# Input projection with 512 moving columns, low parts shared with GpSimd, rotary scores in pairs, output units between head pairs

## The chip, the core and the metric

The kernel runs on one core of a Trainium2 chip. The metric is the device time of one execution in microseconds. Engines are named as in the profile: PE is TensorE's matmul, PEld its weight load, DVE is VectorE, ACT is ScalarE, POOL is GpSimd, SP is SyncE, whose queue issues the weight transfers.

## What is computed

One decoder layer over 256 positions of width 2048, all in float32:

```
x = LN(x)
h = x @ w_in                                   # 2048 -> 2368 columns
c_q, c_kv, k_rope, u_conv, u_pool = split(h)   # 512, 256, 64, 1024, 512
mla:  q = rms(c_q) @ w_uq, kv = rms(c_kv) @ w_ukv, rotary on 64 of 192,
      8 heads, causal softmax, values of 128
conv: a * sigmoid(g) -> causal depthwise conv, 31 taps -> LN -> swish
pool: trailing mean over 2/4/8/16 minus token -> linear per group -> scale
y = concat(mla, conv, pool) @ w_out ;  x = LN(alpha * x + y)
up = causal_conv3(x @ w_up) ; a, g = split(up) ; x = LN(alpha * x + (a * silu(g)) @ w_down)
```

## The kernel before

**Products in three parts.** A large product is made of float32r matmuls: each weight tile and each activation is cut into a high part (its float32r rounding) and a low part (the rest), and hi*hi, hi*lo and lo*hi are added in one PSUM bank. Attention, transposes and statistics use plain float32 matmuls; each of these stands in the trace as two records.

**Weight units.** All weights come as units of 128 x 2048 in a fixed list (`units`): 19 of `w_in` (8 conv, 2 kv, 1 rotary key, 4 q, 4 pool; the first two are used as plain float32), 2 of `w_ukv`, 3 of `w_uq`, 16 of `w_out`, 88 of `w_up`, 44 of `w_down`. A unit is loaded in two halves of 1024 columns. For each half, ScalarE writes the high part (`make_hi`, L198) and VectorE the low part by a subtraction (`make_lo`, L214). `take` hands out the next unit and stages two units further. High and low tiles have six buffers each, three units' worth.

**Input projection.** The channels of x lie in `X`, a tile per k-tile with 256 high and 256 low columns side by side (`X.wide`). `proj` takes for each k-tile and column block three matmuls of 256 moving columns, so that the bank holds the finished sum in its first 256 columns. `proj_wide`, used by the up-projection, takes one matmul over all 512 columns with the high weights, and one of 256 columns with the low weights; the two halves of the bank are added afterwards (`ffn_conv`). In the first unit of a pair it takes the high weights first, in the second the low ones.

**Work in the background.** The 31 taps of each of the four conv groups (L573, L576) go into a queue `bgq`; `bg(n)` takes n of them, and `NBG` sets n after each unit for the conv, kv/q, pool, `w_ukv`/`w_uq` and output units. What is left is done just before `conv_rows`, which transposes the conv groups' results (L818). The angles of the rotary embedding run on GpSimd from a queue of their own (`pq`, `pbg`).

**Attention.** `att_scores(h)` computes the scores of one head and its softmax. The rotary key lies twice, once in rows 0 to 63 (`KA`) and once in rows 64 to 127 (`KB`) with zeros elsewhere, because a tile of rotary queries holds two heads. Two heads ahead of the transposes, the scores are issued; units of the output projection (`wo_unit`) stand between heads in two places. Output units have matmuls of 512 columns; eight banks of PSUM hold everything.

**First residual LayerNorm.** The last three output units are kept; for tokens 0 to 127 they are finished first, then `moments(0)`, and the transposes of the normalised rows (`ln_to_channels`, L277) are woven with the last output matmuls of tokens 128 to 255 (`weave0`). The up-projection's first matmuls (`up_high`, L915) fill the time until the second block's transposes. The reciprocal root of the variance is a power on GpSimd (L263).

**Order.** The program is written in the order in which it is to run; a planner with a cost table orders what is not pinned (`pin`) by readiness and place in the program.

Of the kernel before, what the change touches and what calls it, by code (L numbers as in the profile page):

```python
# [9 lines left out]
F32 = mybir.dt.float32  # L10
# [5 lines left out]
P = 128  # L16
# [22 lines left out]
NBG = (4, 4, 4, 4, 4)  # L39
# [43 lines left out]
def build(tc, ctx, a, out):  # L83
# [77 lines left out]
    wo_order = [(0, 3), (1, 3), (0, 0), (0, 1), (1, 0), (1, 1), (0, 2), (1, 2),  # L161
# [5 lines left out]
    LOOK = 2  # L167
    staged = deque()
# [13 lines left out]
    def stage_load(home=None, raws=None):  # L182
# [8 lines left out]
        for h in range(2):  # L191
# [151 lines left out]
    def m(name="m", dt=F32, w=S):  # L343
        return mp.tile([P, 288], dt, tag="m", name=nm(name), bufs=28)[:, 0:w]
# [169 lines left out]
    def proj(nun, kper, ncb, ah, al, banks, nbg=0, total=None):  # L514
        total = total or nun * kper
        for u in range(nun):
            w = take()
            for k in range(kper):
                kt = u * kper + k
                s0, s1 = kt == 0, kt == total - 1  # L520
                for cb in range(ncb):
                    c = (k * ncb + cb) * P
                    o = banks[cb][:, 0:S]
                    mm(o, w(0, c, P), ah[kt], s0, False)
                    mm(o, w(0, c, P), al[kt], False, False)
                    mm(o, w(1, c, P), ah[kt], False, s1)
            bg(nbg)
            pbg(6)

    def proj_wide(x, xh, banks, nbg=0, u0=0):  # L530
# [10 lines left out]
        for u in range(u0, 2):  # L541
# [10 lines left out]
            bg(nbg)  # L552

    def split_ps(ps, scale, hi, lo):
        act.activation(hi, ps, AF.Identity, scale=scale)
        dve.scalar_tensor_tensor(lo, ps, scale, hi.bitcast(F32), op0=mul, op1=sub)


    accs = []
    for j in range(4):  # L560
        ba, bg_ = first if j == 0 else (bank(), bank())
        if j:
            proj(2, 8, 2, xh, xl, [ba, bg_], nbg=NBG[0])
# [3 lines left out]
        act.activation(sig, bg_[:, 0:S], AF.Sigmoid)  # L567
        dve.tensor_tensor(hp[:, NCONV - 1:NCONV - 1 + S], ba[:, 0:S], sig, op=mul)
# [26 lines left out]
    proj(2, 8, 2, xh, xl, kvb, nbg=NBG[1])  # L595
    kvg, sqs = [], []
    for i in range(2):
        v = m("kvg")
        act.activation(v, kvb[i][:, 0:S], AF.Identity, scale=PC("kv_g", i))
        q = m("sq")  # L600
        act.activation(q, kvb[i][:, 0:S], AF.Square)
        kvg.append(v)
        sqs.append(q)
# [13 lines left out]
    rs_kv = token_rms(sqs, 256)  # L617
    diag = m("diag", w=S)
    for t in range(NTB):
        dve.tensor_scalar(diag[:, t * P:(t + 1) * P], ident, rs_kv[:, t:t + 1], None, op0=mul)  # L620
# [10 lines left out]
    KA = mp.tile([P, S], F32, tag="KA", name="KA")  # L631
    KB = mp.tile([P, S], F32, tag="KB", name="KB")
    pool.memset(KA[64:128], 0.0)
    pool.memset(KB[0:64], 0.0)


    qh, ql, qsq = [], [], []
    for c in range(2):
        qb = [bank(), bank()]
        proj(2, 8, 2, xh, xl, qb, nbg=NBG[1])  # L640
        if c == 0:
# [8 lines left out]
            dve.tensor_tensor(KA[0:64], t0_[0:64], t1_[0:64], op=add)  # L650
            dve.tensor_tensor(KB[64:128], t0_[64:128], t1_[64:128], op=add)
# [10 lines left out]
        for i in range(2):  # L662
            hh, ll = m("cqh", F32R), m("cql", F32R)
            split_ps(qb[i][:, 0:S], PC("q_g", c * 2 + i), hh, ll)
            q = m("sq")
            act.activation(q, qb[i][:, 0:S], AF.Square)
# [10 lines left out]
    def pool_group(gi, b):  # L677
# [4 lines left out]
        act.copy(up[:, PAD:PAD + S], b[:, 0:S])  # L682
# [51 lines left out]
    def q_unit(c):  # L734
        w = take()
        qs = []
        for i in range(4):
# [9 lines left out]
            qs.append(qn)  # L747
        bg(NBG[3])
# [3 lines left out]
    QN += q_unit(1)  # L752
    for i in range(4):
        rope(QR[i], COS, SIN)
# [13 lines left out]
    def att_scores(h):  # L768
        b = bank()
        krr = KA if h % 2 == 0 else KB  # L770
        qr = QR[h // 2]
        mm(b[:, 0:P], QN[h][:, 0:P], KN[h][:, 0:P], True, False)
        mm(b[:, 0:P], qr[:, 0:P], krr[:, 0:P], False, True)
        mm(b[:, P:P + S], QN[h][:, P:S], KN[h], True, False)
        mm(b[:, P:P + S], qr[:, P:S], krr, False, True)
        p = mp.tile([P, 512], F32, tag="p", name=nm("p"), bufs=3)
# [36 lines left out]
    def conv_rows():  # L813

        for t in range(NTB):
# [6 lines left out]
            yn = mp.tile([P, 512], F32, tag="p", name=nm("yn"), bufs=3)  # L822
# [42 lines left out]
    att_scores(0)  # L865
    att_scores(1)
    QN += q_unit(2)
    for i in range(2, H + 4):
        if i < H:
            att_scores(i)  # L870
        if i - 2 < H:
            att_transpose(i - 2)
        if i >= 4:
            att_out(i - 4)
        if i in (4, 7):
            wo_unit(0 if i == 4 else 1)
            bg(NBG[4])
    for i in range(2, 16 - NLAST):
# [51 lines left out]
    for i in range(NLAST):  # L930
# [5 lines left out]
    weave0 = [(1, (2,)), (1, (3,)), (2, (0,)), (2, (1, 2, 3))]  # L936
    ln_to_channels(0, mv, "ln1_g", "ln1_b", X1.pair, lambda w: m("v", w=w),
                   hooks=[(7, f) for f in his0 + his1], weave=lambda kq: last_out(1, weave0[kq][0], ks=weave0[kq][1]))
# [253 lines left out]
```

## Time and profile before

| | |
|---|---|
| median of 3 runs | 1016.16 us (1015.11 to 1016.96) |
| the profiled execution | 1014.3 us, its span 1012.5 us |
| TensorE matmul busy | 1003.0 us, 99% |
| weight loads busy | 884.4 us, 87% |
| VectorE busy | 703.3 us, 69% |
| ScalarE busy | 509.5 us, 50% |
| GpSimd busy | 52.5 us, 5% |
| mean granted TensorE clock | 0.998 |

Times in the trace count from the first instruction. A busy share is an average: which engine sets the end is seen from the chain of work that ended last. Records of matmuls overlap, so the time that a matmul costs is the distance from its start to the next one's start.

### The profile page before, as it was taken

The page shows a single profiled execution, that of the slowest core. Times are in us where ns is not written, and L with a number is a line of the kernel's source. Part 1 is how long each engine was busy: PE and PEld are TensorE (multiplying, and loading weights), DVE is VectorE, ACT ScalarE, POOL GpSimd, SP SyncE. Part 2 cuts the span into 40 slices and gives each one's busy share as a digit, 9 for nine tenths or more (in the row PEclk, how much of TensorE's full clock was granted, in tenths as well). Part 3 has the DMA queues.
Part 4 walks back from the last instruction along what each step waited for, and adds up shares of the span by engine and source line. Part 5 has one row for each costly group of instructions (what it writes and reads, how often), then busy time and mean ns, then how long its engine had stood idle before and what let it go on. Part 6 is the DMA issues. An engine that isn't in the chain of part 4 may idle for free.

```text
span 1012.5 us, 14976 instructions
## 1 busy us (share of the span) xinstructions
PE 1003.0 (99%) x5752; PEld 884.4 (87%) x5752; DVE 703.3 (69%) x1070; ACT 509.5 (50%) x751; POOL 52.5 (5%) x95
## 2 busy tenths in 40 slices
PE   9999999999999999999999999999999999999997
PEld 9999999888898888888888888888888888888885
DVE  6998589987699866666566666666665554554576
ACT  5545466454565654554555455545545444444440
POOL 0830230000000000000000000000000000000000
PEclk9999999999999999999999999999999999999999
DMA  8656444666178656565656555665655766566532
GB/s 322 220 189 197 167 143 148 172 225 206 65 244 253 208 189 197 179 193 189 197 181 195 189 189 188 188 196 181 198 188 191 268 193 204 188 189 201 191 127 84
DMA packets 55656, 193.16 MB, mean 191 GB/s; under 512 B 6432, under 2 KB 6688, under 8 KB 55328
## 3 DMA queue, kind: packets, MB, share of 16 engines
q1 hardware_dynamic: 55152, 191.86, 58.6%
q8 instruction: 45, 0.74, 0.3%
q10 hardware_dynamic: 432, 0.35, 0.1%
q14 instruction: 27, 0.22, 0.1%
HBM read 190.08 MB, written 2.10 MB: 190 GB/s over the span
## 4 chain that ended last, share of the span: by engine, by line
PE 97%; DVE 1%; ACT 1%; DMA 0%; POOL 0%; issue 0%; POOLq 0%; SPq 0%; ACTq 0%
PE ps L256 93%; PE ps L471 1%; PE ps L915 1%; DMA x<-in_x 0%; ACT v L287 0%; PE ps L461 0%; PE ps L586 0%; DVE st L449 0%; PE ps L277 0%; POOL mv L263 0%; PE ps L1069 0%; PE ps L625 0%; PE ps L759 0%; PE ps L1070 0%; DVE st L857 0%; DVE x L856 0%
## 5 line engine op out<-in xcount | busy, mean ns | idle before, releaser
L214 DVE TENSOR_TENSOR lo<-raw,hi 128x1024 fp32r<-128x1024 f32 x340 | 408.6, 1212 | 266.0 <-ACT hi L198 247.3
L198 ACT CAST hi<-raw 128x1024 fp32r<-128x1024 f32 (+1 forms) x342 | 355.4, 1043 | 399.5 <-PE ps L256 366.5
L256 PE MATMUL ps<-x,hi 128*128 128x512 f32 (+1 forms) x1888 | 412.9, 361 | 0.0
L256 PEld LDWEIGHTS ps<-x,hi 128*128 128x128 f32 x1888 | 335.4, 189 | 51.3
L256 PE MATMUL ps<-x,lo 128*128 128x256 f32 x1664 | 248.2, 283 | 0.0
L256 PEld LDWEIGHTS ps<-x,lo 128*128 128x128 f32 x1664 | 223.7, 192 | 3.3
L256 PE MATMUL ps<-hi,al 128*128 128x512 f32 x352 | 136.9, 389 | 0.0
L256 PE MATMUL ps<-hi,ah 128*128 128x512 f32 x352 | 136.9, 389 | 0.0
L256 PE MATMUL ps<-lo,ah 128*128 128x512 f32 x352 | 136.9, 389 | 0.0
L256 PE MATMUL ps<-hi,mx 128*128 128x512 f32 x256 | 81.2, 393 | 0.0
L256 PEld LDWEIGHTS ps<-hi,al 128*128 128x128 f32 x352 | 66.1, 188 | 13.8
L256 PEld LDWEIGHTS ps<-lo,ah 128*128 128x128 f32 x352 | 66.1, 188 | 13.7
L256 PEld LDWEIGHTS ps<-hi,ah 128*128 128x128 f32 x352 | 66.1, 188 | 13.6
L576 DVE SCALAR_TENSOR_TENSOR acc<-hp,pc,acc 128x256 f32<-128x256 f32 x120 | 59.1, 492 | 2.7
L256 PEld LDWEIGHTS ps<-hi,mx 128*128 128x128 f32 x256 | 48.1, 188 | 9.7
L263 POOL TENSOR_TENSOR mv<-mv,cc 128x1 f32<-128x1 f32 x8 | 6.0, 753 | 874.8 <-DVE mv L262 813.5
L256 PE MATMUL ps<-lo,mx 128*128 128x512 f32 x128 | 49.8, 389 | 0.0
L976 ACT COPY u<-ps 128x256 f32<-128x256 f32 x88 | 28.5, 377 | 22.0 <-PE ps L256 21.8
L977 DVE TENSOR_TENSOR u<-ps,u 128x256 f32<-128x256 f32 x88 | 32.9, 415 | 0.0
L256 PEld LDWEIGHTS ps<-lo,mx 128*128 128x128 f32 x128 | 24.1, 188 | 4.7
L978 ACT ACTIVATE ta<-u,pc 128x256 f32<-128x256 f32 x44 | 24.2, 602 | 1.1 <-DVE u L977 1.1
L978 ACT ACTIVATE tg<-u,pc 128x256 f32<-128x256 f32 x44 | 24.1, 600 | 0.1
(181 smaller groups left out, 662.0 us busy)
## 6 DMA issues: line engine op xcount, KB each, us to landing
raw<-in_w_up SPq DMA_DIRECT2D x174, 512.0 KB, 4.3
raw<-in_w_down SPq DMA_DIRECT2D x88, 512.0 KB, 4.2
raw<-in_w_in SPq DMA_DIRECT2D x34, 512.0 KB, 4.3
raw<-in_w_out SPq DMA_DIRECT2D x32, 512.0 KB, 4.5
raw<-in_w_uq SPq DMA_DIRECT2D x6, 512.0 KB, 4.0
x<-in_x SPq DMA_DIRECT2D x8, 256.0 KB, 5.4
plain<-in_w_in SPq DMA_DIRECT2D x4, 512.0 KB, 7.2
raw<-in_w_ukv SPq DMA_DIRECT2D x4, 512.0 KB, 4.1
```

What stands on the lines that cost most here:

```text
L198: i_ = act.copy(hi, raw[:, o:o + wd])
L214: i_ = dve.tensor_tensor(lo, raw[:, o:o + wd], w.parts[0][len(w.parts[1])].bitcast(F32), op=sub)
L256: pe.matmul(o, l, r, start=start, stop=stop)
L263: pool.tensor_tensor(mv[:, 2:3], mv[:, 1:2], nhalf[:, 0:1], op=ALU.pow)
L471: pin(pe.matmul(first[cb][:, t * P:(t + 1) * P], plain[kt // 8](((kt % 8) * 2 + cb) * P, P), vx[c][:, j, t * P:(t + 1) * P], start=kt == 0 ...
L576: dve.scalar_tensor_tensor(acc, hp[:, k:k + S], PC("conv_w", j * NCONV + k), acc, op0=mul, op1=add)
L915: pin(pe.matmul(token_block(ub[u // 2 * 2 + cb], t), us[u](0, up_col(kt, cb), P), token_block(X1.wide(kt), t), start=t == 0 and kt % 16 == ...
L976: act.copy(u, ps[:, S:2 * S])
L977: dve.tensor_tensor(u, ps[:, 0:S], u, op=add)
L978: act.activation(t_, u, AF.Identity, scale=PC("ffn_w", 2 * 2 * NF + blk), bias=PC("ffn_b", blk))
```

## The change

The conv (three of four groups), kv, q and pool projections use `proj_wide` and `halves`, which copies the second half of the bank and adds it to the first; `proj` goes. The low part of the second half of units 9 to 29 is computed by GpSimd. The kv statistics are taken in the middle of the first q projection. The four squares of q are added by GpSimd before one product with ones. The rotary key lies in one tile `KR`, its two copies in rows 0 to 63 and 64 to 127, and the rotary scores of two heads are products of 64 rows each. The rope of the queries runs between the heads of the next query unit. Scores and softmax go by pairs of heads, an output unit stands before each pair's transposes from the second pair on, and the order of two output units is swapped. In the first residual LayerNorm the output matmuls go behind the first two transposes, and one low part moves behind the fourth pair of channels. Scratch tiles `m` are 27 instead of 28, softmax tiles `p` 4 instead of 3.

```
-NBG = (4, 4, 4, 4, 4)
+NBG = (4, 5, 6, 4, 4)
-    wo_order = [(0, 3), (1, 3), (0, 0), (0, 1), (1, 0), (1, 1), (0, 2), (1, 2),
+    wo_order = [(0, 3), (1, 3), (0, 0), (1, 0), (0, 1), (1, 1), (0, 2), (1, 2),
+    POOL_LO = range(9, 30)
-            def make_lo(raw=raw, h=h, late=True):
+            def make_lo(raw=raw, h=h, late=True, eng=pool if h and nxt[0] - 1 in POOL_LO else dve):
-                    i_ = dve.tensor_tensor(lo, raw[:, o:o + wd], w.parts[0][len(w.parts[1])].bitcast(F32), op=sub)
+                    i_ = eng.tensor_tensor(lo, raw[:, o:o + wd], w.parts[0][len(w.parts[1])].bitcast(F32), op=sub)
-        return mp.tile([P, 288], dt, tag="m", name=nm(name), bufs=28)[:, 0:w]
+        return mp.tile([P, 288], dt, tag="m", name=nm(name), bufs=27)[:, 0:w]
-    def proj(nun, kper, ncb, ah, al, banks, nbg=0, total=None):
...
-    def proj_wide(x, xh, banks, nbg=0, u0=0):
+    def proj_wide(x, xh, banks, nbg=0, u0=0, npq=0, between=None):
...
             bg(nbg)
+            pbg(npq)
+            if u == 0 and between is not None:
+                between()
+    xw = [X.wide(k) for k in range(KT)]
+    def halves(b, dst=None):
+        t_ = m("half")
+        act.copy(t_, b[:, S:2 * S])
+        dst = t_ if dst is None else dst
+        dve.tensor_tensor(dst, b[:, 0:S], t_, op=add)
+        return dst
-            proj(2, 8, 2, xh, xl, [ba, bg_], nbg=NBG[0])
+            proj_wide(xw, xh, [ba, bg_], nbg=NBG[0], npq=6)
...
+        gate, val = (halves(bg_), halves(ba)) if j else (bg_[:, 0:S], ba[:, 0:S])
+        act.activation(sig, gate, AF.Sigmoid)
+        dve.tensor_tensor(hp[:, NCONV - 1:NCONV - 1 + S], val, sig, op=mul)
-    rs_kv = token_rms(sqs, 256)
...
+    def kv_diag():
+        rs_kv = token_rms(sqs, 256)
+        for t in range(NTB):
+            dve.tensor_scalar(diag[:, t * P:(t + 1) * P], ident, rs_kv[:, t:t + 1], None, op0=mul)
...
-        proj(2, 8, 2, xh, xl, qb, nbg=NBG[1])
+        proj_wide(xw, xh, qb, nbg=NBG[1], npq=6, between=kv_diag if c == 0 else None)
-            dve.tensor_tensor(KA[0:64], t0_[0:64], t1_[0:64], op=add)
-            dve.tensor_tensor(KB[64:128], t0_[64:128], t1_[64:128], op=add)
+            dve.tensor_tensor(KR, t0_, t1_, op=add)
...
-        proj(2, 8, 2, xh, xl, pb, nbg=NBG[2])
+        proj_wide(xw, xh, pb, nbg=NBG[2], npq=6)
         if c == 0:
-            rs_q = token_rms(qsq, 512)
+            for q in qsq[1:]:
+                pool.tensor_tensor(qsq[0], qsq[0], q, op=add)
+            rs_q = token_rms(qsq[0:1], 512)
...
-    QN += q_unit(1)
-    for i in range(4):
-        rope(QR[i], COS, SIN)
+    QN += q_unit(1, lambda i: rope(QR[i], COS, SIN))
...
+    def att_scores(h0):
+        hs = (h0, h0 + 1)
+        for h in hs:
+            SB[h] = bank()
+            mm(SB[h][:, 0:P], QN[h][:, 0:P], KN[h][:, 0:P], True, False)
+            mm(SB[h][:, P:P + S], QN[h][:, P:S], KN[h], False, False)
+        qr = QR[h0 // 2]
+        for o, q, nk in ((slice(0, P), slice(0, P), P), (slice(P, P + S), slice(P, S), S)):
+            for i, h in enumerate(hs):
+                r = slice(i * 64, (i + 1) * 64)
+                pin(pe.matmul(SB[h][:, o], qr[r, q], KR[r, 0:nk], start=False, stop=o.start == P))
...
+    def softmaxes(h0):
+        att_scores(h0)
+        att_softmax(h0)
+        att_softmax(h0 + 1)
+    softmaxes(0)
     QN += q_unit(2)
...
+    for h in range(0, H, 2):
+        if h + 2 < H:
+            softmaxes(h + 2)
+        if h:
+            wo_unit(h // 2 - 1)
             bg(NBG[4])
+        att_transpose(h)
+        att_transpose(h + 1)
+        if h:
+            att_out(h - 2)
+            att_out(h - 1)
+    att_out(H - 2)
+    att_out(H - 1)
-    for i in range(2, 16 - NLAST):
+    for i in range(3, 16 - NLAST):
...
-    weave0 = [(1, (2,)), (1, (3,)), (2, (0,)), (2, (1, 2, 3))]
+    def weave0(kq):
+        if kq == 0:
+            last_out(1, 1, ks=(2, 3))
+        elif kq == 1:
+            last_out(1, 2)
...
-    los0[0]()
...
-                   hooks=[(3, los0[1]), (7, los1[0]), (7, los1[1]), (7, los2[0]), (7, los2[1])], weave=weave1)
+                   hooks=[(3, los0[0]), (3, los0[1]), (7, los1[0]), (7, los1[1]), (7, los2[0]), (7, los2[1])], weave=weave1)
```

## Rows read from the trace of the kernel before

**Rows 1.** The page's first part: busy time, share of span, instructions.
```profile
PE 1003.0 (99%) x5752; PEld 884.4 (87%) x5752; DVE 703.3 (69%) x1070; ACT 509.5 (50%) x751; POOL 52.5 (5%) x95
```

**Rows 2.** The chain that ended last: start us, us, engine, line, count.
```profile
91.84 23.03 PE ps L256 x192
114.87 1.68 PE ps L586 x16
...
195.12 0.87 PE ps L818 x8
```

**Rows 3.** Timeline of TensorE in the up-projection, us 300 to 312: start, us, instructions merged.
```profile
302.77 7.44 PE L256 MATMUL ps<-x,hi 128*128 128x512 f32 x32
310.05 2.19 PE L256 MATMUL ps<-x,lo 128*128 128x256 f32 x17
```

**Rows 4.** Timeline of TensorE at the first heads' scores.
```profile
154.34 0.39 PE L256 MATMUL ps<-KA,qn 128*128 128x128 f32 x2
154.56 0.60 PE L256 MATMUL ps<-kn,qn 128*128 128x256 f32 x2
154.99 0.59 PE L256 MATMUL ps<-KA,qn 128*128 128x256 f32 x2
155.43 0.38 PE L256 MATMUL ps<-kn,qn 128*128 128x128 f32 x2
...
156.55 0.47 PE L256 MATMUL ps<-cqh,hi 128*128 128x256 f32 x1
156.85 0.28 PE L256 MATMUL ps<-cql,hi 128*128 128x256 f32 x1
```

**Rows 5.** Timelines of TensorE and of VectorE at the first pair.
```profile
27.27 0.48 PE L256 MATMUL ps<-x,hi 128*128 128x256 f32 x2
...
31.72 3.69 DVE L214 TENSOR_TENSOR lo<-raw,hi 128x1024 fp32r<-128x1024 f32 x3
```

**Rows 6.** Busy time from 60 to 195: all, of tile lo, of tile acc.
```profile
60.00:195.00 135.00, 135.00 (x993) 128.29 (x992) 117.04 (x257) 74.24 (x143) 16.18 (x30) 1.00 0.51 161
...
60.00:195.00 135.00, 77.53 (x262) 49.75 (x262) 44.94 (x38) 1.00 0.51 161
...
60.00:195.00 135.00, 0.04 (x1) 0.18 (x2) 48.73 (x101) 1.00 0.51 161
```

**Rows 7.** Timeline of VectorE: low parts and conv taps.
```profile
75.11 3.08 DVE L576 SCALAR_TENSOR_TENSOR acc<-hp,pc,acc 128x256 f32<-128x256 f32 x6
78.11 2.35 DVE L214 TENSOR_TENSOR lo<-raw,hi 128x1024 fp32r<-128x1024 f32 x2
...
129.22 2.88 DVE L576 SCALAR_TENSOR_TENSOR acc<-hp,pc,acc 128x256 f32<-128x256 f32 x4
```

**Rows 8.** Timeline of GpSimd at the pool groups' sums.
```profile
118.86 0.62 POOL L687 TENSOR_TENSOR ws<-up 128x258 f32<-128x258 f32 x1
...
128.36 1.43 POOL L687 TENSOR_TENSOR ws<-up 128x262 f32<-128x262 f32 x1 [7.34 <-ACT up L682]
129.87 1.44 POOL L687 TENSOR_TENSOR ws<-ws 128x260 f32<-128x260 f32 x2
```

**Rows 9.** Timelines of GpSimd, VectorE and TensorE at the first residual LayerNorm.
```profile
261.52 0.55 POOL L263 TENSOR_TENSOR mv<-mv,cc 128x1 f32<-128x1 f32 x1 [61.77 <-DVE mv L262]
272.48 1.39 POOL L263 TENSOR_TENSOR mv<-mv,cc 128x1 f32<-128x1 f32 x1 [10.41 <-DVE mv L262]
...
272.24 1.22 DVE L214 TENSOR_TENSOR lo<-raw,hi 128x1024 fp32r<-128x1024 f32 x1
...
269.35 3.99 PE L915 MATMUL ps<-x,hi 128*128 128x256 f32 x32
274.50 0.66 PE L277 MATMUL ps<-cc,x 128*128 128x128 f32 x4 [1.17 <-DVE x L272]
```

**Rows 10.** Timeline of VectorE at the last conv taps.
```profile
190.95 3.09 DVE L576 SCALAR_TENSOR_TENSOR acc<-hp,pc,acc 128x256 f32<-128x256 f32 x6
```

**Rows 11.** The page's fifth part: a group of instructions, busy us, mean ns.
```profile
L977 DVE TENSOR_TENSOR u<-ps,u 128x256 f32<-128x256 f32 x88 | 32.9, 415 | 0.0
```

More of the change, by code (lines that the diff above doesn't have):

```diff
@@ L511, in build @@
     res_in = residual_ops(dve, a["ln_in_g"], a["ln_in_b"])
-    def proj(nun, kper, ncb, ah, al, banks, nbg=0, total=None):
[L515 to L528, printed above, removed]
-    def proj_wide(x, xh, banks, nbg=0, u0=0):
+    def proj_wide(x, xh, banks, nbg=0, u0=0, npq=0, between=None):
         def high(w, kt, last):
@@ L594, in build @@
     kvb = [bank(), bank()]
-    proj(2, 8, 2, xh, xl, kvb, nbg=NBG[1])
+    proj_wide(xw, xh, kvb, nbg=NBG[1], npq=6)
     kvg, sqs = [], []
     for i in range(2):
+        kv = halves(kvb[i])
         v = m("kvg")
-        act.activation(v, kvb[i][:, 0:S], AF.Identity, scale=PC("kv_g", i))
+        act.activation(v, kv, AF.Identity, scale=PC("kv_g", i))
         q = m("sq")
-        act.activation(q, kvb[i][:, 0:S], AF.Square)
+        act.activation(q, kv, AF.Square)
         kvg.append(v)
@@ L615, in build @@
     cs_ = cos_sin()
-    rs_kv = token_rms(sqs, 256)
     diag = m("diag", w=S)
-    for t in range(NTB):
-        dve.tensor_scalar(diag[:, t * P:(t + 1) * P], ident, rs_kv[:, t:t + 1], None, op0=mul)
+    def kv_diag():
+        rs_kv = token_rms(sqs, 256)
+        for t in range(NTB):
+            dve.tensor_scalar(diag[:, t * P:(t + 1) * P], ident, rs_kv[:, t:t + 1], None, op0=mul)
     def rope(src, cos, sin):
@@ L629, in rope @@
         dve.tensor_tensor(src, src, t1, op=add)
[L631 to L634, printed above, removed]
+    KR = mp.tile([P, S], F32, tag="KA", name="KR")
     qh, ql, qsq = [], [], []
@@ L663, in build @@
             hh, ll = m("cqh", F32R), m("cql", F32R)
-            split_ps(qb[i][:, 0:S], PC("q_g", c * 2 + i), hh, ll)
+            qs_ = halves(qb[i])
+            split_ps(qs_, PC("q_g", c * 2 + i), hh, ll)
             q = m("sq")
-            act.activation(q, qb[i][:, 0:S], AF.Square)
+            act.activation(q, qs_, AF.Square)
             qh.append(hh)
@@ L681, in pool_group @@
         pool.memset(up[:, 0:PAD], 0.0)
-        act.copy(up[:, PAD:PAD + S], b[:, 0:S])
+        halves(b, up[:, PAD:PAD + S])
         cur, wdt = up, 1
@@ L733, in build, with q_unit @@
     bg(NBG[3])
-    def q_unit(c):
+    def q_unit(c, between=None):
         w = take()
@@ L747, in q_unit @@
             qs.append(qn)
+            if between is not None:
+                between(i)
         bg(NBG[3])
@@ L766, in build, with att_softmax @@
     SC, PT = {}, {}
[L768 to L776, printed above, removed]
+    SB = {}
+    def att_scores(h0):
[9 more added lines that the diff above has]
+                pin(pe.matmul(SB[h][:, o], qr[r, q], KR[r, 0:nk], start=False, stop=o.start == P))
+    def att_softmax(h):
+        b = SB.pop(h)
+        p = mp.tile([P, 512], F32, tag="p", name=nm("p"), bufs=4)
         sm = small(name="smx")
@@ L821, in conv_rows @@
             mv = ln_stats_finish(st, 1, t)
-            yn = mp.tile([P, 512], F32, tag="p", name=nm("yn"), bufs=3)
+            yn = mp.tile([P, 512], F32, tag="p", name=nm("yn"), bufs=4)
             dve.tensor_scalar(yn, b, mv[:, 0:1], mv[:, 2:3], op0=sub, op1=mul)
@@ L863, in wo_unit @@
             wo_mm(n, kg, w, t, kg == 3, False)
-    att_scores(0)
-    att_scores(1)
-    QN += q_unit(2)
[L868 to L876, printed above, removed]
-            bg(NBG[4])
-    for i in range(2, 16 - NLAST):
+    def softmaxes(h0):
[3 more added lines that the diff above has]
+    softmaxes(0)
+    QN += q_unit(2)
+    for h in range(0, H, 2):
[3 more added lines that the diff above has]
+            wo_unit(h // 2 - 1)
+            bg(NBG[4])
+        att_transpose(h)
[6 more added lines that the diff above has]
+    for i in range(3, 16 - NLAST):
         n, kg = wo_order[i]
@@ L935, in build @@
     last_out(1, 1, ks=range(2))
-    weave0 = [(1, (2,)), (1, (3,)), (2, (0,)), (2, (1, 2, 3))]
+    def weave0(kq):
[3 more added lines that the diff above has]
+            last_out(1, 2)
     ln_to_channels(0, mv, "ln1_g", "ln1_b", X1.pair, lambda w: m("v", w=w),
-                   hooks=[(7, f) for f in his0 + his1], weave=lambda kq: last_out(1, weave0[kq][0], ks=weave0[kq][1]))
+                   hooks=[(7, f) for f in his0 + his1], weave=weave0)
     for f in his2:
```

2 lines of the change are left out of this document (removed).

## The prediction

> **What bounds the kernel now.** I read the page first, then the chain that ended last, then timelines of single engines. TensorE is busy 99% of the span [rows 1], and the chain is a nearly unbroken row of its matmuls: 192 in 23.03 us, then sixteen small ones in 1.68 us, and so on [rows 2]. The reader is to see that only two things shorten this time: less TensorE work, or removal of one of its few waits. Inside the body I find one wait above 0.5 us: the transposes of the second token block at the first residual LayerNorm, 1.17 us idle [rows 9]. VectorE and GpSimd matter only if they come too late.
>
> **Input projection.** Before, each k-tile and column block takes three matmuls of 256 moving columns; 192 take 23.03 us, 0.120 each [rows 2]. After, one of 512 and one of 256. The up-projection already has both shapes: 32 of 512 columns start 7.28 us apart in all, 0.2275 each [rows 3]. So 0.3475 takes the place of 0.360, 0.0125 less. There are 8 projections (three conv, one kv, two q, two pool) of 16 k-tiles and 2 blocks, 256 such triples: **-3.2 us**. These are columns of the same number; what goes is one issue of three. I see no unknown in it.
>
> The new order has a cost. In a pair's second unit the low parts come first now. The first pair's matmuls begin at 27.27, so its second unit's begin 5.56 us later, at 32.83; but three low parts run on VectorE from 31.72 to 35.41 [rows 5], and the first two belong to that unit. They end, a third of the stretch each, at about 33.0 and 34.2, while TensorE wants them at 32.8 and, eight matmuls on, at 33.8. **+0.5 us** (0 to 0.6); later units are further ahead.
>
> **Halves added.** Sixteen additions on VectorE, each like the up-projection's 415 ns [rows 11], and as many copies on ScalarE (four replace others). They sit behind a bank that TensorE does not need at once, since the next pair takes other banks. Nothing on the path; VectorE gets 10 x 0.34 (one after another they overlap a little) = 3.4 us more between 60 and 195 us.
>
> **Sums of squares of q.** Sixteen records at 1.68 us [rows 2] become four: **-1.26 us**. GpSimd adds the four tiles while the first pool projection runs (11 us of matmuls); its three additions, 0.62 each at 258 columns [rows 8], end long before. The kv statistics move into the middle of the first q projection, with 5.5 us of matmuls before the result is used; the chain behind them is some 2 us plus one low part on GpSimd. Nothing on the path.
>
> **Rotary scores.** Now two heads share a zero-padded 128-row product each. From 154.34 to 154.56 the 128-column part takes 0.22, from 154.99 to 155.43 the 256-column part 0.44 [rows 4]: 0.66 per head, 5.25 us for eight. After, two heads' products use rows 0-63 and 64-127. No row shows 64-row products. Bounds: two halves wholly at once, -2.6; one after the other, 0, plus eight changes of shape. For a change of shape the nearest row is the first low-precision matmul behind the scores, 0.30 instead of 0.12 [rows 4], 0.18; eight would be +1.4. Each f32 product is two records, issued in order: with first-head-first order only the second record of one head can meet the first of the other, so I take a third, -1.75, less eight half-priced changes, 0.7: **-1.0** (-2.6 to +1.4).
>
> The Trainium skill ("TensorE: Matmul & The Clock Gate", Part 3) says that matmuls in distinct row groups run concurrently, starting some 4 ns apart; by it this term would be the full -2.6. Its page "TensorEngine Tiling (Array Packing)", Key Properties, says that a change of tiling mode drains the engine, which speaks the other way; no row here shows either.
>
> **Rope between query heads.** The same eight records, but three more returns from f32 to the low/high products, each up to 0.18 [rows 4]: **+0.4**. One more output unit between heads adds one return, **+0.1**. The output units move to where TensorE would wait for softmax: each is 5.4 us of cover. VectorE's softmax for a pair is about 4 us, so no wait is expected in the attention.
>
> **LayerNorm weave.** The output matmuls of block 1 now end before the third and fourth transposes, not after, so its moments start some 0.9 us earlier. And the low part that ran from 272.24 no longer stands beside GpSimd's power: that took 1.39 us, against 0.55 where nothing stood beside it [rows 9]: 0.84 back. Together 1.7, more than the wait, which is 1.3 against the normal spacing (269.35 and 32 matmuls of 0.12 make 273.2; the transposes start at 274.50). Two alternations of kind fewer, 0.15. The low part goes behind the fourth pair, where TensorE has 32 matmuls of 0.12 before it needs it. What is late next is ScalarE, whose fifth pair waits 0.2 us for the third transpose; the last pair had 0.7 us in hand. **-1.45** (-1.5 to 0).
>
> **Low parts on GpSimd.** Twenty halves of units 9 to 29 (unit 10 has none of this kind) leave VectorE, where two in a row take 2.35, 1.13 each [rows 7]: 22.7 us less. But the two engines do not work beside each other. A GpSimd addition at 128.36 took 1.43, one alone 0.62 [rows 8]; the power above waited out a whole low part [rows 9]. And in return, four conv taps at 129.22 took 2.88 us where six undisturbed take 3.08, so four take 2.05 [rows 7]: 0.83 lost to three additions of about 260 columns, 0.28 each. A low part has 1024 columns: at least 4 x 0.28 = 1.1 us taken from VectorE, at most 4 x 0.62 = 2.5. I take 1.3, near the taps, since the fixed cost is paid once. It is lost only where VectorE wants the shared port: low parts and taps are 44.94 and 48.73 of its 117.04 us from 60 to 195 [rows 6], 0.80.
>
> The deadline is the transposition of the conv rows at 195.12 [rows 2]; the last tap ended at 190.95 + 3.09 = 194.04 [rows 10], 1.1 us ahead. TensorE will be there about 4.7 us earlier, so 130.3 us are to be had. Demand: 117.0 - 22.7 + 3.4 + 20 x 0.8 x 1.3 = 118.5, and some 5 us of gaps that no work can fill (18.0 are idle now; the earlier taps by the larger background counts fill others): 123.5. It fits: **0**. The path of a single low part fits too: the second low part of the pair at 78.11 ends at 80.46 [rows 7] for a unit that starts at 91.84 [rows 2], 11 us ahead; 3 us more do not show.
>
> Sum: -3.2 + 0.5 - 1.26 - 1.0 + 0.4 + 0.1 - 1.45 = **-5.9 us**. The profiled execution, 1014.3 us (span 1012.5 and 1.8 around it), becomes 1008.4. It lay 1.9 below the median 1016.16; from that median the forecast is **1010.3 us**.
>
> **Rivals.**
> (a) The port. At price p per low part VectorE needs 117.0 - 22.7 + 3.4 + 5 + 16p. Above p = 1.7 it passes 130.3 and TensorE waits for the conv rows; above p = 2.1 the wait eats the whole 5.9; at p = 2.5 it is 12.4 and the time 1016.2 + 6.5 = 1022.7. For it: VectorE is now idle mostly in places that other things held up, and taps end only 1.1 us ahead. Against it: 0.28 per 260 columns. Chance 0.14 for slower, and 0.2 for a wait of 2 to 8 us (1012 to 1018). The Trainium skill ("GPSIMD Engine Reference", section 3.1) gives 4497 ns for 2048 columns against VectorE's 2293, so by estimate 2.25 us here; by that price (a) would hold, with a wait of 8.4 us and 1018.7. Its section 1 states the shared interface; the trace agrees in kind (1.43 against 0.62 us), and its 258 columns in 0.62 us do not decide the price at 1024.
> (b) The rotary pairs do not overlap, and changes of shape cost in full: -5.9 + 1.0 + 1.4 = -3.5, 1012.7. For it: no row shows any overlap of matmuls. Chance 0.15.
> (c) The wait at the LayerNorm only moves, to ScalarE's fifth pair: -4.6, 1011.5; within the forecast's own range.
> (d) 27 instead of 28 scratch tiles, with sixteen short-lived more, hold up an eviction until a bank is missing: no worth; chance 0.06, about 1016.
>
> **Numbers.** The forecast 0.45 (own range 1007 to 1012), (b) 0.15, (a) small 0.2, large 0.14, (d) 0.06. A measurement tells 0.2%, 2 us, from no change. Faster: 0.45 + 0.15 + half of 0.2 = 0.69 rounded; same: the rest of (a) small and half of (d), 0.14; slower 0.17. The lower end takes rotary at its best and no new wait: 1007. The upper end leaves out the dearest part of (a): 1018.
>
> **What would show it.** Matmuls of 512 and 256 columns at 0.2275 and 0.12 in the input projection; four records of the q statistics; a TensorE gap near 33 us of half a microsecond; no gap before the second LayerNorm's transposes, and a power of 0.55 us; GpSimd's low parts of 1.7 to 3 us with VectorE's taps stretched beside them. It is wrong if TensorE waits in front of the conv rows, or for a GpSimd low part, or if the 64-row products leave gaps.

## The result, and the profile after

| | before | after |
|---|---|---|
| median | 1015.63 us | 1039.75 us (1039.16 to 1042.26, 4 runs) |
| ratio after / before, 95% interval | | 1.0237 [1.0213, 1.0261] |
| the profiled execution, its span | 1014.3, 1012.5 us | 1042.26, 1040.4 us |

The change makes the kernel 24 us slower; forecast were 1010.3 us and a range that ended at 1018. The profiles here also differ at the start: where the fourth of eight chunks of x landed by 6.84 us, TensorE's first high product started at 27.1 to 27.7 (27.27 in the profile of before), and where it landed from 7.22 to 9.70, at 29.0 to 31.7 (31.02 in that of after). Shifts of a place in the program are therefore given from that first product on: the last matmul of the down-projection in after is 24.09 us late by it.

The page's first part, after [rows 1]:

```profile
PE 1008.0 (97%) x5484; PEld 874.6 (84%) x5484; DVE 719.9 (69%) x1065; ACT 512.1 (49%) x763; POOL 101.2 (10%) x116
```

TensorE has 268 matmuls fewer and is busy 5 us longer. VectorE gave away twenty subtractions and is busy 16.6 us longer. The page's fourth part says where the chain now runs; before, it was a row of matmuls [rows 2]:

```profile
PE 85%; DVE 9%; issue 3%; POOL 1%; DMA 1%; ACT 0%; POOLq 0%; ACTq 0%; DVEq 0%
PE ps L257 80%; DVE acc L575 6%; DVE lo L215 2%; PE ps L472 2%; PE ps L932 1%; POOL ws L686 1%; DMA x<-in_x 1%; PE ps L462 0%; DMA cc<-in_consts 0%; PE ps L782 0%; DVE cql L544 0%; PE ps L760 0%; PE ps L278 0%; POOL lo L215 0%; DVE half L553 0%
```

Conv taps (L575) are on the chain with 6% of the span. The view of TensorE's waits (line that waited, what it waited for, us in total, times, longest) names the places:

```profile
PE ps L760 <- DVE t L629: 8.3, 1, 8.3
PE ps L257 <- DVE up L553: 5.9, 1, 5.9
PE ps L585 <- ACT sq L601: 3.3, 2, 1.7
PE ps L651 <- DVE diag L622: 2.9, 1, 2.9
...
PE ps L932 <- DVE x L294: 1.2, 3, 0.6
```

Before, this view has nothing between 60 and 195 us. Now TensorE waits for a rotary product that VectorE has not read (L629), for the half sums of a pooled pair (L553), for the squares of kv (behind half sums) and for their diagonal (L622): four results that VectorE owes soon after TensorE has given it the input. None of the four is a low part (one wait of 0.4 us is for one, which VectorE made itself). The second one in TensorE's timeline, and two stretches of the windows view (span of the stretch, then busy us and instructions of PE, PEld, DVE, ACT, POOL, then granted clock, DMA share, GB/s):

```profile
140.90 0.28 PE L257 MATMUL ps<-ckl,hi 128*128 128x256 f32 x1
141.02 0.28 PE L257 MATMUL ps<-ckh,lo 128*128 128x256 f32 x1
147.17 0.58 PE L257 MATMUL ps<-ckh,hi 128*128 128x256 f32 x1 [5.87 <-DVE up L553]
...
147.97 0.41 PE L257 MATMUL ps<-ckh,hi 128*128 128x256 f32 x1
148.19 0.41 PE L257 MATMUL ps<-ckl,hi 128*128 128x256 f32 x1
```
```profile
91.00:94.00 3.00, 3.00 (x16) 3.00 (x16) 2.89 (x4) 2.86 (x4) 2.01 (x1) 0.50 0.36 139
...
147.00:153.00 6.00, 5.83 (x21) 5.23 (x22) 5.20 (x7) 4.26 (x9) 5.46 (x8) 0.56 0.48 171
```

Behind the wait a matmul of 256 columns takes 0.21 us instead of 0.12: the granted clock is at its lower level, 1.2 of 2.4 GHz. So such a wait is paid twice: this one, the one of 8.3 us and the two that make 3.3 us were followed by a stretch at the lower clock, the one of 2.9 us was not. The four add up to 20.4 us; by estimate, busy time by missing clock, summed over the stretches 87 to 94, 147 to 153 and 180 to 184, is some 6.6 us more (5.83 x 0.44 = 2.6 in the second).

Why VectorE is late is seen where GpSimd's low parts run. First GpSimd's timeline, then the chain from 91 us on (start us, us, what):

```profile
91.99 5.15 POOL L215 TENSOR_TENSOR lo<-raw,hi 128x1024 fp32r<-128x1024 f32 x2 [10.12 <-ACT hi L199]
...
99.09 2.58 POOL L215 TENSOR_TENSOR lo<-raw,hi 128x1024 fp32r<-128x1024 f32 x1 [0.56 <-ACT hi L199]
```
```profile
91.87 0.50 DVE acc L575
92.39 2.50 DVE acc L575
94.92 2.52 DVE acc L575
...
99.52 2.44 DVE acc L575
101.96 0.40 DVE diag L622 x2
...
102.50 0.67 PE ps L651 x2
```

A tap that takes 0.50 us takes 2.5 when it starts beside a low part on GpSimd: it ends about when the low part does. VectorE loses 2.0 us each time. It goes the other way too: where a low part on VectorE was already under way, GpSimd's took 2.82 to 3.22 us instead of 2.34 to 2.61 (three cases). Of the twenty low parts, sixteen have a stretched instruction of VectorE (2.4 to 2.7 us; one of 1.8) beside them; fourteen of these are taps. The other four ran from 194 us on, beside instructions like these (GpSimd, then VectorE):

```profile
202.79 2.37 POOL L215 TENSOR_TENSOR lo<-raw,hi 128x1024 fp32r<-128x1024 f32 x1 [6.09 <-ACT hi L199]
```
```profile
203.79 0.42 DVE L819 TENSOR_TENSOR mx<-ps,mx 128x256 fp32r<-128x256 f32 x1 [0.96 <-ACT mx L818]
204.46 0.42 DVE L819 TENSOR_TENSOR mx<-ps,mx 128x256 fp32r<-128x256 f32 x1 [0.24 <-ACT mx L818]
```

These read one operand from PSUM, lie wholly inside a low part, and take their usual 0.42 us. The Trainium skill ("GPSIMD Engine Reference", section 1) names the contention so: with VectorE's instructions that have two SBUF inputs. The trace agrees: 2.5 us with two, 0.42 with one.

What the rest of the change did, in rows. The projection's matmuls [rows 2, 3], the rotary scores of a pair with what follows them [rows 4], and the first LayerNorm on GpSimd and TensorE [rows 9]:

```profile
61.31 7.44 PE L257 MATMUL ps<-x,hi 128*128 128x512 f32 x32
68.59 3.63 PE L257 MATMUL ps<-x,lo 128*128 128x256 f32 x29
...
191.98 0.93 PE L782 MATMUL ps<-KR,qn 64*128 64x128 f32 x8
192.84 0.33 PE L803 MATMUL ps<-cc,p 128*128 128x128 f32 x1
...
299.83 0.73 PE L932 MATMUL ps<-x,hi 128*128 128x256 f32 x4 [0.64 <-DVE x L294]
300.92 0.71 PE L932 MATMUL ps<-x,hi 128*128 128x256 f32 x4 [0.35 <-DVE x L294]
```
```profile
298.31 0.55 POOL L264 TENSOR_TENSOR mv<-mv,cc 128x1 f32<-128x1 f32 x1 [8.92 <-DVE mv L263]
```

32 matmuls of 512 columns take 7.28 us from the first start to the next kind, 0.2275 each, as forecast. Eight rotary records of a pair take 0.86 us (191.98 to 192.84) against 1.31 for two heads. A narrower view, 191.95 to 192.05, shows how:

```profile
191.67 0.38 PE L257 MATMUL ps<-kn,qn 128*128 128x256 f32 x1
191.98 0.38 PE L782 MATMUL ps<-KR,qn 64*128 64x128 f32 x2
```

The records start in twos, 0.006 to 0.007 us apart (191.98, 192.19, 192.30, 192.52), so two products of 64 rows run at once. That alone would make 0.66 of 1.31. The rest is paid at the two changes of shape, on both sides of them: the last 128-row record ahead stands for 0.31 instead of 0.22 us and the first two of 64 rows for 0.21 instead of 0.11; the last two of 64 rows stand for 0.31 instead of 0.22 and the 128-row record behind them (192.84 to 193.00) for 0.16 instead of 0.11.

The power takes 0.55 instead of 1.39 us. But where one wait of 1.17 us stood ahead of the second block's transposes, TensorE now waits three times for pairs of the first.

### The profile page after: what moved, and what is told of

Read it like the earlier page. It is cut to its first block, busy times and chain, and to the rows that moved or that the text cites. A ratio compares the mean times of both kernels' runs of the same rounds, so it can differ in the third digit from the quotient of the medians.

```text
span 1040.4 us, 14466 instructions
## 1 busy us (share of the span) xinstructions
PE 1008.0 (97%) x5484; PEld 874.6 (84%) x5484; DVE 719.9 (69%) x1065; ACT 512.1 (49%) x763; POOL 101.2 (10%) x116
## 4 chain that ended last, share of the span: by engine, by line
PE 85%; DVE 9%; issue 3%; POOL 1%; DMA 1%; ACT 0%; POOLq 0%; ACTq 0%; DVEq 0%
PE ps L257 80%; DVE acc L575 6%; DVE lo L215 2%; PE ps L472 2%; PE ps L932 1%; POOL ws L686 1%; DMA x<-in_x 1%; PE ps L462 0%; DMA cc<-in_consts 0%; PE ps L782 0%; DVE cql L544 0%; PE ps L760 0%; PE ps L278 0%; POOL lo L215 0%; DVE half L553 0%
## 5 line engine op out<-in xcount | busy, mean ns | idle before, releaser
L215 DVE TENSOR_TENSOR lo<-raw,hi 128x1024 fp32r<-128x1024 f32 (+1 forms) x320 | 384.1, 1211 | 264.4 <-ACT hi L199 246.2
L257 PE MATMUL ps<-x,hi 128*128 128x512 f32 x1632 | 380.7, 390 | 0.0
L257 PEld LDWEIGHTS ps<-x,hi 128*128 128x128 f32 x1632 | 303.2, 188 | 60.7
L257 PEld LDWEIGHTS ps<-x,lo 128*128 128x128 f32 x1664 | 208.1, 193 | 4.3 <-DVE lo L215 0.4
L257 PE MATMUL ps<-x,lo 128*128 128x256 f32 x1664 | 210.1, 284 | 0.0
L575 DVE SCALAR_TENSOR_TENSOR acc<-hp,pc,acc 128x256 f32<-128x256 f32 x120 | 88.2, 735 | 2.9
L215 POOL TENSOR_TENSOR lo<-raw,hi 128x1024 fp32r<-128x1024 f32 x20 | 51.0, 2555 | 76.4 <-ACT hi L199 76.2
```

Source lines behind the costliest of these rows:

```text
L215: i_ = eng.tensor_tensor(lo, raw[:, o:o + wd], w.parts[0][len(w.parts[1])].bitcast(F32), op=sub)
L257: pe.matmul(o, l, r, start=start, stop=stop)
L575: dve.scalar_tensor_tensor(acc, hp[:, k:k + S], PC("conv_w", j * NCONV + k), acc, op0=mul, op1=add)
```

## The experiments

Each experiment is a kernel of its own, e1 to e14; a ratio is its time over that of the kernel before, with the 95% interval in brackets.

**1. GpSimd's share taken out, alone and with pieces of the rest undone.** Kernels e1, e2, e3 and e4 ran beside each other.

e1: the changed kernel, low parts on VectorE.

```diff
-    POOL_LO = range(9, 30)
+    POOL_LO = ()
```

> The changed kernel with every low part on VectorE again. Theory A (the port: each low part on GpSimd keeps VectorE's two-input instructions waiting for some 2 us, and VectorE is late for TensorE from 60 us on): the waits of TensorE for VectorE go, conv taps take 0.49 us in the mean again instead of 0.735, and the time falls by 25 to 30 us to about 1011, below the kernel before. Theory B (the halves, the wider background counts and the 27 scratch tiles make VectorE late, whoever does the low parts): VectorE has 22.7 us more to do, so the time stays above 1030.

e2: the kernel before with that share as the only change.

```diff
+    POOL_LO = range(9, 30)
-            def make_lo(raw=raw, h=h, late=True):
+            def make_lo(raw=raw, h=h, late=True, eng=pool if h and nxt[0] - 1 in POOL_LO else dve):
...
-                    i_ = dve.tensor_tensor(lo, ...)
+                    i_ = eng.tensor_tensor(lo, ...)
```

> The kernel before with the second low parts of units 9 to 29 on GpSimd and nothing else. Theory A: it is slower than before by 10 us or more, with taps at 0.7 us and waits of TensorE for VectorE. Theory B: within 3 us of before, since VectorE is relieved of 22.7 us and has no halves to add.

e3: the changed kernel, each of GpSimd's low parts in four instructions of 256 columns.

```diff
-                    i_ = eng.tensor_tensor(lo, ...)
...
+                    st_ = 256 if eng is pool else wd
+                    for q_ in range(0, wd, st_):
+                        i_ = eng.tensor_tensor(lo[:, q_:q_ + st_], ...)
```

> The changed kernel with GpSimd's low parts in four pieces of 256 columns each. Theory A: the port is held for the same sum of columns, but VectorE gets in between the pieces; a tap waits 0.5 us at most instead of 2, and the time falls by 5 to 20 us, to 1020 to 1035. If only the total held counts, no change beyond 3 us. Theory B: no change.

e4: e1 with the old weave at the first LayerNorm.

```diff
+    weave_ = [(1, (2,)), (1, (3,)), (2, (0,)), (2, (1, 2, 3))]
     def weave0(kq):
-        if kq == 0:
...
+        last_out(1, weave_[kq][0], ks=weave_[kq][1])
     mv = moments(1)
+    los0[0]()
...
```

> As the first of this call (no low part on GpSimd), with the old order at the first residual LayerNorm. By the prediction's step the new order is worth 1.45 us, so this one is slower than the first by 1.5 us; by the trace of the changed kernel, where three waits of 1.7 us in all have taken the place of one of 1.2, the two are within 0.5 us of each other.

Measured, with ratios to the kernel before: e1 1017.58 us, 1.0013 [0.9995, 1.0032]; e2 1028.28, 1.013 [1.0101, 1.0159]; e3 1033.35, 1.0179 [1.0151, 1.0207]; e4 1016.76, 1.0002 [0.9985, 1.002]. The taps' group in each (busy us, mean ns, idle before), e1, e2, e3 in this order, and e3's low parts:

```profile
L575 DVE SCALAR_TENSOR_TENSOR acc<-hp,pc,acc 128x256 f32<-128x256 f32 x120 | 58.4, 491 | 1.9
```
```profile
L577 DVE SCALAR_TENSOR_TENSOR acc<-hp,pc,acc 128x256 f32<-128x256 f32 x120 | 82.6, 688 | 3.0
```
```profile
L578 DVE SCALAR_TENSOR_TENSOR acc<-hp,pc,acc 128x256 f32<-128x256 f32 x120 | 75.7, 631 | 2.9
...
L218 POOL TENSOR_TENSOR lo<-raw,hi 128x256 fp32r<-128x256 f32 x80 | 70.5, 908 | 62.7 <-ACT hi L199 47.9 <-PE ps L808 14.7
```

Without GpSimd's share the 22 us are back and a tap takes its old 491 ns. The share alone makes the kernel before 13 us slower: VectorE is relieved of 20.0 us of low parts (408.6 to 388.6) and loses 23.5 on the taps (59.1 to 82.6); its view of waits names other results than that of the changed kernel (a low part 4.0 us, an output's low part 2.8, a softmax tile 1.4, a rotated query 1.2). Pieces of 256 columns give 6 us back and cost GpSimd 3.6 us a low part instead of 2.55. So GpSimd's share, by what it holds up on VectorE, is the main cause; but e1 is no faster than before either. In its trace the query products come 4.03 us early, just what projection and squares should give; at the last pooled product 1.1 are left, behind a wait of 1.8 us for a rotary product (L760 for L629) and a slow clock. e4 differs from e1 by less than its interval; in the traces, the stretch from the first LayerNorm's first transposes to the up-projection's low parts costs e1 0.58 us against before, e4 nothing.

**2. Rotary turns back where they were, counts, and GpSimd on top.** e5: e4 with the rope behind the second query unit.

```diff
-    QN += q_unit(1, lambda i: rope(QR[i], COS, SIN))
+    QN += q_unit(1)
+    for i in range(4):
+        rope(QR[i], COS, SIN)
```

> No low part on GpSimd, the old order at the first residual LayerNorm, and the rope of the queries behind the query unit as before; the other parts of the change stay. Theory A (what is left of the loss in the first experiment is TensorE's wait at the pool groups' products for a bank that a rope product holds until VectorE gets to it): no wait there, the gain of about 4 us up to the query units stays and the scores add 1 us, so 4 to 6 us below before: ratio 0.994 to 0.997. Rival: the pairing of the heads itself costs the time, by transitions between kinds of matmul; then it stays within 1.5 us of before.

e6: the changed kernel with `NBG = (4, 4, 4, 4, 4)`.

> The changed kernel with four conv taps after each unit everywhere, as before. Theory A (the port): taps still meet GpSimd's low parts, so within 4 us of the changed kernel. Rival C (the wider background counts put taps in front of what TensorE waits for): 8 us or more below the changed kernel.

e7: e5 with `POOL_LO = range(9, 30)`.

> As the first of this call, but with the low parts of units 9 to 29 on GpSimd again. Theory A: VectorE falls behind as before, so 12 us or more above the first of this call; the wait of 8 us at the pool groups' products is smaller, since the rope products stand elsewhere, so 5 to 10 us below the changed kernel. If the loss depended on the rope's place alone, it would be within 3 us of the first of this call.

e8: e5, in which GpSimd repeats its twenty subtractions over the loaded weights once both parts are made. VectorE computes every low part; nothing reads what GpSimd writes.

```diff
...
                     w.parts[1].append(lo)
+                    if h and u_ in range(9, 30):
+                        pool.tensor_tensor(raw[:, o:o + wd], raw[:, o:o + wd], w.parts[0][...].bitcast(F32), op=sub)
```

> As the first of this call, all low parts on VectorE, and beside them GpSimd repeats the subtraction for the second halves of units 9 to 29, with its result written over the loaded weights that nothing reads any more: GpSimd's load of the port without any relief for VectorE. Theory A with a price of 2.0 us for each: VectorE loses up to 40 us and is late everywhere, 20 us or more above the first of this call. With the price of the prediction, 1.3 us: VectorE loses 21 us at 0.8, of which gaps swallow about half: 8 to 14 us above.

Measured: e5 1017.71, 1.0028 [1.0012, 1.0044]; e6 1040.57, 1.0246 [1.022, 1.0272]; e7 1043.33, 1.0278 [1.0248, 1.0308]; e8 1051.27, 1.0353 [1.0324, 1.0382]. The counts are no cause of the 24 us: e6 is where the changed kernel is. Work on GpSimd that relieves nobody and that nobody reads costs 34 us over e5, with the taps at 725 ns. Not all of that is VectorE's loss: one wait of 4.8 us is for GpSimd's own sum of the squares of q, which stands behind a repeated subtraction in GpSimd's queue, and the loaded weights are held longer, though no wait of TensorE's there is for a part of a weight. e7 lies 25 us over e5, but missed on its place: 3.6 us above the changed kernel instead of 5 to 10 below; its wait for a rotary product stands at the scores and takes 11.7 us instead of 8.3. e5 missed what I expected: the wait at the pooled products went, and another came at the scores. In e5's timelines of TensorE and VectorE:

```profile
148.42 1.89 PE L762 MATMUL ps<-dd,wp 128*128 128x256 f32 x8
155.50 2.93 PE L257 MATMUL ps<-kn,qn 128*128 128x128 f32 x8 [5.19 <-DVE t L629]
```
```profile
148.09 2.35 DVE L215 TENSOR_TENSOR lo<-raw,hi 128x1024 fp32r<-128x1024 f32 x2
150.37 3.60 DVE L575 SCALAR_TENSOR_TENSOR acc<-hp,pc,acc 128x256 f32<-128x256 f32 x7
153.89 1.22 DVE L215 TENSOR_TENSOR lo<-raw,hi 128x1024 fp32r<-128x1024 f32 x1
155.02 0.42 DVE L629 TENSOR_TENSOR t<-ps,cs 128x256 f32<-128x256 f32 x1
```

The scores need a bank that a rotary product still holds. VectorE reads it only at 155.02, because low parts and seven taps stand ahead of it in its queue, and nobody needs the taps' sums for 40 us. From the first high product on, TensorE makes the first rotary product 3.94 us earlier than before, and VectorE reads it 2.80 us later (127.79 against 124.99).

**3. The taps moved.** e9: e5 with `NBG = (4, 6, 8, 0, 4)`. e10: e5 with

```diff
-NBG = (4, 5, 6, 4, 4)
+NBG = (4, 5, 6, 0, 6)
```

e11: as e9, with the rope between the first query unit and the second. e12: e1 with e10's counts, that is the changed kernel with two tuples altered.

> The version with rotary turns after both query units, old LayerNorm order and no low part on GpSimd, with the background taps issued sooner: 6 instead of 5 after a key or query piece, 8 instead of 6 after a pooled piece, none after the four up-projections. In that version VectorE stood 5.2 us late at the scores (149.93 to 155.50) with taps and low parts in front of the rotary products. Theory A (the saving of 4 us is real and only the taps in front of the rotary products eat it): 16 taps of 0.48 us fewer stand there, the 5.2 us wait and the clock's fall behind it go, and the time is 4 to 6 us under the kernel before (1008.5 to 1011). Theory B (VectorE is full from 56 us on, 76.4 of 84 us busy between 56 and 140, so that taps set earlier only make an earlier result late): another wait of 2 to 5 us appears before 140 us, and the time is within 2 us of the kernel before.

> The same version with no taps after the four up-projections and 6 instead of 4 after each output unit: the 16 taps go later, to the head pairs and ahead of the convolution rows. Theory A: the wait at the scores goes; VectorE had 6.4 us idle between 180 and 195, which takes most of 7.7 us of taps; the conv rows wait at most 1 us; 4 to 6 us under the kernel before. Theory B (VectorE has no room left before the conv rows): TensorE waits 3 us or more for the accumulators near 195, and the gain is under 2 us.

> As the version with taps sooner, and the rotary turns issued right behind the first query unit, ahead of the second. Theory A: the rotary products are read 4 us sooner by TensorE's time, so no wait is left at the scores or the pooled products; 4 to 6 us under the kernel before, equal to the version with taps sooner if that has no wait left. Theory B: as TensorE gets to the rotary products sooner, VectorE is still late there and the wait stands at the pooled products (1 to 3 us), and the gain is under 2 us.

> The changed kernel with two tuples altered: no low part on GpSimd, and the background taps taken away behind the four up-projections and set behind the output units instead (0 and 6 for 4 and 4). Its rotary turns stay between the heads of the second query unit and its LayerNorm order stays new. Theory A (only the taps in front of the rotary products ate the saving, wherever these stand): the 1.9 us wait at the pooled products and the slow clock behind it go, and the time is that of the version with taps late plus about 0.55 us for the new LayerNorm order: 4 to 5 us under the kernel before. Theory B (rotary turns between heads are late in themselves, as TensorE meets their products earlier): a wait of 1 us or more stands at the second query unit or the pooled products, and the time is within 2.5 us of the kernel before.

Measured: e9 1019.95, 1.0043 [1.0028, 1.0058]; **e10 1011.76, 0.9954 [0.9937, 0.9971]**; e11 1016.85, 1.0005 [0.999, 1.002]; e12 1012.9, 0.9977 [0.9963, 0.9991]. VectorE in e10 at the place where e5 waits:

```profile
146.32 3.49 DVE L215 TENSOR_TENSOR lo<-raw,hi 128x1024 fp32r<-128x1024 f32 x3
150.91 1.23 DVE L215 TENSOR_TENSOR lo<-raw,hi 128x1024 fp32r<-128x1024 f32 x1 [1.11 <-ACT hi L199]
152.06 0.42 DVE L629 TENSOR_TENSOR t<-ps,cs 128x256 f32<-128x256 f32 x1
```

No tap stands there, the rotary product is read at 152.06, and TensorE does not wait at the scores. The 4 us stay; 4.92 are there at the conv rows' first transpose, 4.6 at the last matmul of the down-projection. e10 beats both kernels, the one before by 0.3 to 0.6%. e9 missed: asked for sooner, taps still stood in VectorE's queue from 147.46 to 156.3, since the planner decides the order, and TensorE waited 6.4 us. e11 shows no wait for a rotary product, but TensorE stands 1.1 us for a half sum and 2.6 at the pooled products, there for nothing that the profile shows. e12 came out between its theories: the wait at the pooled products is gone (3.90 us kept there), but 0.8 us go at one wait for an output's low part and 2.2 at the LayerNorm. The view names there the same three waits as in e1, 1.25 us in all; the stretch costs e1 0.58. In e12 a stretch at the lower clock follows them, in e1 none:

```profile
273.00:277.00 4.00, 4.00 (x25) 4.00 (x23) 1.53 (x6) 2.44 (x7) 0.00 (x0) 0.57 0.00 0
```

By estimate that is 4.00 x 0.43 = 1.7 us, the rest of the 2.2.

**4. Is the price enough by itself, and whose is the gain?** e13: e10 with `POOL_LO = range(9, 30)`. e14: the kernel before with `NBG = (4, 4, 4, 0, 6)`.

> The version with taps late (4.6 us under the kernel before by its ratio), and GpSimd's twenty low parts put back, nothing else. Theory A (the port's price alone is enough: about 2.0 us of VectorE for each low part in place of the 1.13 to 1.22 that the subtraction itself takes): VectorE, busy 40.77 of 41.20 us from 153.8 to 195, has no room left; TensorE waits at several places and the time is 12 us or more over the kernel before. Theory B (the port only hurts because taps stand in front of the rotary products): with the taps behind them the loss is small, and the time is within 4 us of the kernel before.

> The kernel before with the background taps alone moved late (0 instead of 4 behind the four up-projections, 6 instead of 4 behind the output units). Theory A (the gain of the version with taps late is that of the projection, the squares and the rotary pairs, and the taps only stop eating it): the kernel before has no wait between 60 and 195 us, so moving taps gives nothing: within 1 us, or slower by a wait ahead of the conv rows. Theory B (the order of the taps is a gain by itself): 2 us or more faster.

Measured: e13 1038.35, 1.0233 [1.0207, 1.0258]; e14 1014.29, 0.9993 [0.9977, 1.0008]. e13's waits, its low parts on GpSimd, and VectorE from 60 to 195 [rows 6]:

```profile
PE ps L257 <- DVE up L553: 5.6, 1, 5.6
PE ps L257 <- DVE mx L821: 3.9, 1, 3.9
PE ps L651 <- DVE diag L622: 3.8, 1, 3.8
PE ps L585 <- ACT sq L601: 3.5, 2, 2.0
```
```profile
L215 POOL TENSOR_TENSOR lo<-raw,hi 128x1024 fp32r<-128x1024 f32 x20 | 52.8, 2647 | 73.1 <-ACT hi L199 63.5 <-PE ps L257 9.3
```
```profile
60.00:195.00 135.00, 121.61 (x724) 106.58 (x723) 118.48 (x212) 68.23 (x130) 70.18 (x68) 0.96 0.41 143
```

With the rotary products out of the taps' way GpSimd's share still costs 27 us, at other places. VectorE is not full there (118.48 of 135 us): it is late for single results, not for its sum of work. And the taps' place is worth nothing to the kernel before, so e10's gain is that of the other parts that it keeps, by the forecast's terms the projection, the squares and the pairs.

## Why the prediction was wrong, by its steps

**"I take 1.3, near the taps": the price of a low part, failed.** It was chosen between 1.1 and 2.5 by the three short additions of rows 8, each of which took 0.28 us from the taps. The whole instruction counts: VectorE stands for as long as the low part runs, 2.4 to 2.6 us, less its own 0.5, so 2.0. The share of 0.8 came out, sixteen of twenty. With 0.8 x 2.0 = 1.6 against 1.13 for doing it itself [rows 7], a low part handed to GpSimd leaves VectorE with less time, not more; at that price the step is ruled out, whatever the deadline. The Trainium skill ("GPSIMD Engine Reference", section 3.1) led by estimate to 2.25 us for the low part; measured were 2.34 to 2.61 where no low part of VectorE's was under way, so the page's price was near. The prediction weighed that price as a rival and gave "slower" a chance of 0.14.

**"The deadline is the transposition of the conv rows", failed.** By the prediction's own sum, a price of 2.0 asks for 134.7 of 130.3 us, so a wait of 4.4 and still a gain of 1.5. Measured were 22 us between the changed kernel and e1, and none of it in front of the conv rows. In the changed kernel VectorE is busy only 7.82 of 18.00 us ahead of the conv rows (205 to 223):

```profile
205.00:223.00 18.00, 18.00 (x111) 15.50 (x112) 7.82 (x26) 10.03 (x22) 4.91 (x3) 1.00 0.55 157
```

Its queue runs in order. Each result that TensorE wants soon is a deadline of its own, and the taps, put there as filling, stand ahead of it. Rival (a) had the right engine and direction with the wrong place and size.

**"Halves added: nothing on the path" and "kv statistics: nothing on the path", failed with GpSimd's share.** The half sums (5.9 us), the squares behind half sums (3.3) and the diagonal (2.9) are three of the four great waits. Without that share they cost nothing (e10), as forecast; but the half sums (forecast as 3.4 us) and the taps of the larger counts do fill VectorE: 76.46 of 84 us busy from 56 to 140 in e10, 67.96 before. That may be why e2 loses 13 us to GpSimd's share and the changed kernel 22, but it is not shown: e6, with the old counts, loses as much as the changed kernel, and the half sums were not tried alone.

**Rope between heads, "+0.4": failed as a cost of return.** At the first pooled product e1, with the turns between heads, is 3.93 us ahead of before, and e5, with the turns behind the unit, 3.94: the three returns cost nothing. The 0.18 for one was read from one distance alone. The records ahead of it, in the kernel before:

```profile
156.30 0.59 PE L256 MATMUL ps<-KB,qn 128*128 128x256 f32 x2
```

Their second starts at 156.52, and the next matmul 0.03 us after it, at 156.55 [rows 4]. What that one has too much, the record ahead of it has too little: 156.30 to 156.85 is 0.55, as twice 0.22 and 0.12 are. The rows that mattered were VectorE's: the rotary product is read late (e1), and behind the second unit likewise (e5), until the taps go (e10, e12).

**LayerNorm weave, "-1.45": failed, much as rival (c) had it, but at another place.** The power came back to 0.55 us as said, and the wait moved to the first block's pairs, with VectorE's low halves (L294) last, not ScalarE. From the first block's transposes to the up-projection's low parts it costs 0.5 to 0.6 us (changed kernel, e1), and 2.2 with the lower clock behind it (e12), where 1.45 should have come back.

**Right:** the projection, the squares and the wait near 33 us: -3.2 - 1.26 + 0.5 = -3.96 forecast, -4.01 to -4.03 measured at the query products in e1, e5 and e10. In the first pair 32 low-part matmuls take 4.33 us from start to start, in the next 3.83: the wait of 0.5.

**Right by luck: the rotary pairs, "-1.0".** From the pooled products to the conv rows e10 gains 0.98. But the forecast took a third for the overlap, 1.75, less 0.7 for eight changes of shape at 0.09. The records show the overlap whole, 2.6, as in the prediction's own bound, and by estimate 0.15 to 0.2 us for each change, 1.5 for eight, so -1.1: two errors that cancel. The rule of "TensorE: Matmul & The Clock Gate", Part 3, in the Trainium skill, by which the halves run wholly at once, starting some 4 ns apart, agrees with these records (6 to 7 ns); the price of the changes comes on top of it.

**The sum.** The sum without the weave and the rope between heads, -5.9 + 1.45 - 0.4 = -4.85, is what e10, which has neither nor GpSimd's share, shows: -4.7 by its ratio (interval -6.4 to -2.9), -4.6 in its trace; the part of the pairs in it is the luck just named.

Open stays why the planner leaves taps ahead of the rotary products when they are asked for sooner (e9); its costs were not changed. Open too is why the changed kernel loses 9 us more to GpSimd's share than e2, and which part of e8's 34 us is due to weights held longer.

## What to carry to other kernels

Before work goes to GpSimd, ask what VectorE's two-input instructions lose while it runs, and compare that with what VectorE would spend on the work itself; here 2.0 us in sixteen of twenty cases against 1.13. For an engine with an in-order queue, list every result that another engine wants within a few us, and what filling stands ahead of each, instead of one sum against the last deadline. When a price is read from the distance between two starts, add the distance ahead of it before you believe it. When TensorE is made faster, look at the queues it now meets earlier: the same 16 taps moved behind the rotary turns made the difference between no gain (e5) and 4.7 us (e10).

## What was unexpected of the hardware

While GpSimd runs one subtraction of 1024 columns (two SBUF inputs), a VectorE instruction with two SBUF inputs that starts beside it stands for its whole length (0.50 to 2.5 us), and one with an operand in PSUM is not held at all (0.42 us). Cutting GpSimd's instruction in four costs GpSimd 1.1 us a low part and frees VectorE only in part (taps 631 instead of 735 ns). Waits of 3.3 us (two together), 5.9 and 8.3 on TensorE were each followed by a stretch at the lower clock, worth another 1.5 to 2.6 us by estimate; one of 2.9 was not, and three of 1.25 us together were in one kernel (e12, 1.7 us more) and not in another (e1). Products of 64 rows of two heads ran wholly at once, their records 6 to 7 ns apart, and each change between 64 and 128 rows took 0.15 to 0.2 us.
